# Queries of the second layer copied out into four buffers, and the out projection's weights asked for behind the first bias rows

## The chip, the cores and the metric

The kernel runs on one NeuronCore of a Trainium2 chip. The metric is the device time of one execution in microseconds (us). Three runs of the kernel before gave 2109.16, 2102.2 and 2106.66 us, median 2106.66 us.

## What is computed

The reference runs a model of two blocks over 1024 tokens of width 1024. The first block has an even layer (windowed attention and a state-space mixer) and an odd layer; a second block follows (state-space, convolution and a gated embedding). The change lies in the odd layer, called the second layer here:

```python
def odd_layer(hn, rel_bias, w_in, w_out, q_g, k_g):
    q, k, v, gate, qi, ki, wi = split_cols(hn @ w_in, ODD_SPLITS)
    q = rms_norm(q.reshape(bsz, L, C_HEADS, C_HEAD_DIM), q_g)
    k = rms_norm(k.reshape(bsz, L, C_KV_HEADS, C_HEAD_DIM), k_g)
    ...
    att = dsa_attention(q, k, v, qi, ki, wi, rel_bias)
    return (att * jax.nn.silu(gate)) @ w_out
```

There are 8 query heads and 2 key heads of 128. For each token a small indexer (qi, ki, wi) scores all earlier keys; the 256 best are kept, and the attention's logits (with a bias that depends on the distance) are masked to those. All of it is in float32.

## The kernel before

float32 products are made of three matmuls each on split operands (`mm3`, L146 to L150: high by high, high by low, low by high), so the lines L148, L149 and L150 come in threes on PE. Weights come in pieces of 128x512 (`wpiece`, L103): a load into one of three `wraw` buffers (L110, on SP), the high part by ACT (L122), the low part by POOL (L123). `wchunk` (L143) asks for eight of them.

The order of the instructions on each engine and of the DMAs on SP is found by the tile scheduler, which ranks what is ready by priority; `high_priority(offset=WPRIO)` lifts the weights' pieces (L106), the query loads (L1138) and the bias rows (L1164). Every engine, and SP as an issuer of DMAs, works through its list in order: what waits at its head holds all that is behind it.

The second layer (phase b, L835 to L1007) goes through these stages:

- Indexer scores into `sc2` to `sc7`, one row of scores for each block of 128 queries from the third on. Then the gate projection; its result goes through two buffers (tag "gt" in the pool `xp`, L926) to DRAM (`d_gate`). Then keys and values.
- The query projection (L958 to L967): two halves of 512 columns, eight token tiles each, 24 matmuls to a tile out of `hnTB`. After each tile comes `head_norm(..., leave=True)` (L400 to L410): ACT copies the PSUM bank out into `qo` (L401, two buffers, tag "qo"), squares its four heads (L404); POOL forms the reciprocal root and scales (L405, L168, L407) and stores the tile to `d_q` in DRAM (L409). A copy-out buffer is free again when its store has landed. In the second half the banks are three "tp" and one "mm" in turn (L963).
- Beside the query projection runs the choice of the 256 best (`TopK`): 31 steps of bisection. For the blocks 5, 6 and 7 a step is a small DVE operation (L1074), a Sign over the row of scores by ACT (L1078), and two small DVE operations (L1082, L1083). At the end DVE makes the mask (L1113 to L1123), a prefix scan (L1120) the longest piece of it.
- The pool `xp` is closed (L974) and `b_dsa_e` is opened over its space; `hnTB` is closed (L977), and `b_mix` (with `mixB`, L980), `b_ms` and `b_dsa` are opened over its space. So `mixB` waits for the last matmul that reads `hnTB`, and what lies in `b_dsa_e` waits for what lay in `xp`.
- The out projection's weights `wo` are asked for (L983), and the attention runs as a pipeline of 16 units, a block of queries by a key head (L985, blocks in the order 0, 1, 7, 6, 5, 4, 3, 2). A unit's `front` (L1149) loads its queries (`qf`, L1139, one buffer), turns them by four PE transposes (`tq`, L1143) into `qTB` (L1145 on ACT, L1146 on DVE), loads a row of biases for each of its four heads (`lgB`, L1165; the first two heads' buffers lie in `b_dsa_e`, the other two in `b_dsa`), makes the scores on PE (`s<-kTB,qTB`), adds the bias and takes the maximum on DVE (L1174), and normalises by ACT (L1178, L1180). Its `back` (L1183) transposes the weights (`tp`, L1192), multiplies by the values (`po`), loads the gate's 128x4x128 piece into `mixB` (L1199), and multiplies (L1200, DVE). The front of unit i+1 stands ahead of the back of unit i (L195 to L197).
- Both units of a block done, `out_tile` (L1010) splits `mixB` into `ms` (L1021, L1022), multiplies by `wo`, loads the block's 512 columns of x (`xr`, L1026, into the buffer with the tag "sq" that the squares of `head_norm` use), adds and stores.

Of the kernel before, what the change touches and what calls it, by code (L numbers as in the profile page):

```python
# [11 lines left out]
F32 = mybir.dt.float32  # L12
# [7 lines left out]
P = 128  # L20
# [32 lines left out]
def dap(ap, offset, pattern):  # L53
    return bass.AP(tensor=ap.tensor, offset=ap.offset + offset, ap=[list(p) for p in pattern])
# [135 lines left out]
def pipeline(att, units, done):  # L190

    late = None
    att.front(*units[0])
    for i, u in enumerate(units):
        if isinstance(att, DSA) and i + 1 < len(units):  # L195
            att.front(*units[i + 1])
        att.back(*u)  # L197
        if isinstance(att, SWA) and i + 1 < len(units):
            att.front(*units[i + 1])
        if late is not None:  # L200
            done(late)
            late = None
        if u[1] == 1:
            late = u[0]
    done(late)
# [183 lines left out]
def head_norm(k, pool, ps, nh, dh, dst, leave=False, o=None):  # L389

    nc = k.nc
    V, S, G = nc.vector, nc.scalar, nc.gpsimd
    n = nh * dh
    if o is None:
        o = pool.tile([P, 512], F32, tag="qo", name="qo", bufs=2)[:, :n]
    m = pool.tile([P, 16], F32, tag="hm", name="hm")
    r = pool.tile([P, 16], F32, tag="hr", name="hr")
    h3 = lambda a: a.rearrange("p (h d) -> p h d", h=nh)
    sq = pool.tile([P, 512], F32, tag="sq", name="sq", bufs=1)
    if leave:  # L400
        S.activation(o, ps, AF.Copy)  # L401
        for h in range(nh):
            hs = slice(h * dh, h * dh + dh)
            S.activation(sq[:, hs], o[:, hs], AF.Square, accum_out=m[:, h:h + 1])  # L404
        G.tensor_scalar(m[:, :nh], m[:, :nh], 1.0 / dh, 1e-6, op0=ALU.mult, op1=ALU.add)  # L405
        k.rstd(r[:, :nh], m[:, :nh], nh)
        G.tensor_tensor(h3(o), h3(o), r[:, :nh].unsqueeze(2).to_broadcast([P, nh, dh]), op=ALU.mult)  # L407
        if dst is not None:
            nc.gpsimd.dma_start(dst, o)  # L409
        return o  # L410
    S.activation(sq[:, :n], ps, AF.Square)
    V.tensor_reduce(m[:, :nh], h3(sq[:, :n]), axis=AX.X, op=ALU.add)
    V.tensor_scalar(m[:, :nh], m[:, :nh], 1.0 / dh, 1e-6, op0=ALU.mult, op1=ALU.add)
    k.rstd(r[:, :nh], m[:, :nh], nh)
    V.tensor_tensor(h3(o), h3(ps), r[:, :nh].unsqueeze(2).to_broadcast([P, nh, dh]), op=ALU.mult)  # L415
    if dst is not None:
        nc.sync.dma_start(dst, o)
    return o
# [416 lines left out]
def phase_b(k, x, hout, hB):  # L835
    hnT, sL = hB
    nc, tc, ins = k.nc, k.tc, k.ins
    V, S, G, T = nc.vector, nc.scalar, nc.gpsimd, nc.tensor
    W = ins["od_w_in"][0]
    d_q = tc.dram_tile([L, D], F32, name="d_q")  # L840
# [3 lines left out]
    gp = sR.enter_context(k.pool("b_g", side="right"))  # L844
# [11 lines left out]
    ps = k.tp()  # L856
# [8 lines left out]
    for th in range(2):  # L865
        cs = slice(th * 512, th * 512 + 512)
        ps = k.mm()
# [8 lines left out]
        ps = k.tp()  # L876
# [6 lines left out]
        for m in range(4):  # L883
            ps = k.mm()
# [5 lines left out]
            for e in range(2):  # L890
                a, b = slice(e * 64, e * 64 + 64), slice(64 - e * 64, 128 - e * 64)
# [8 lines left out]
    for b in range(2, 8):  # L900
        n = (b + 1) * P
# [18 lines left out]
    for ch in range(2):  # L920
        wg = k.wchunk(W, 1536 + ch * 512, 512)
        for m in range(4):
            for th in range(2):
                ps = k.mm()
                k.form2(ps, hnT, th * 512, wg, KT, m * P)
                gt = xp.tile([P, 512], F32, tag="gt", name="gtB", bufs=2)  # L926
# [15 lines left out]
    def keys(tt):  # L942
        ts_ = slice(tt * P, (tt + 1) * P)
        pt = k.tp()
        with tc.issue_after(k.last.ins):
            for j in range(2):
                T.transpose(pt[:, j * P:(j + 1) * P], kraw(tt)[:, j * P:(j + 1) * P], k.ident)
        src = pt[:, :256].rearrange("p (a t) -> p a t", a=2)
        S.activation(kT[:, 0, :, ts_], src, AF.Copy, scale=kg[:, 1:2])
        V.scalar_tensor_tensor(kT[:, 1, :, ts_], src, kg[:, 1:2], kT[:, 0, :, ts_].bitcast(F32),  # L950
                               op0=ALU.mult, op1=ALU.subtract)
    for tt in range(NT):
        ps = k.mm()
# [4 lines left out]
    for ch in range(2):  # L958
        wq = k.wchunk(W, ch * 512, 512)
        if ch:  # L960
            k.psum(mm=1,s=3,po=1,tp=3)
        for tt in range(NT):
            ps = k.ps(("tp", "tp", "tp", "mm")[tt % 4] if ch else "mm", "mm")  # L963
            k.form1(ps, hnT, tt * P, wq, KT, 512)
            if ch == 0:
                keys(tt)
            head_norm(k, gp, ps, 4, 128, d_q[tt * P:(tt + 1) * P, ch * 512:ch * 512 + 512], True)  # L967
    tks = [TopK(k, xp, sc, bs, act) for bs, act in TOPK]
    for bit in range(30, -1, -1):
        for t in tks:  # L970
# [7 lines left out]
    Wo = ins["od_w_out"][0]  # L978
    sL, (mp, mo) = stack(k.pool("b_mix"), k.pool("b_ms"))
    mix = mp.tile([P, 8, L], F32, name="mixB")  # L980
    with ExitStack() as c2:
        dp = c2.enter_context(k.pool("b_dsa"))
        wo = k.wchunk(Wo, 0, 512)  # L983
        ds = DSA(k, ep, dp, d_q, d_T, d_gate, kT, vB, sc, kg, mix)
        units = [(b, kv) for b in DORD for kv in range(2)]  # L985
        pipeline(ds, units, lambda b: out_tile(k, mo, gp, b, 0, [mix], wo, x, hout, "sq", 1))
    sR.close()
    k.wdve = WDVE[3]
# [10 lines left out]
    wo = [k.wpiece(Wo, kk, [(512, 512)], pool=op if kk < 4 else None, nx=4) for kk in range(KT)]  # L999
    for tt in range(NT):  # L1000
        h = out_tile(k, mo, op, tt, 1, [mix], wo, x, hout)
# [8 lines left out]
def out_tile(k, mo, p, tt, ch, mixes, w, x, hout, xtag="xr", nx=2, bank="mm"):  # L1010

    nc = k.nc
    V, S, G, T = nc.vector, nc.scalar, nc.gpsimd, nc.tensor
    ts_ = slice(tt * P, (tt + 1) * P)
    n = len(mixes)
    ps = k.ps(bank, "mm")
    for i in range(2):
        m = mo.tile([P, 2, 4, P], F32R, tag="ms", name="ms", bufs=MSB)
        with k.tc.high_priority(offset=2 * WPRIO if ch else 0):
            mx = mixes[i % n][:, (4 * i if n == 1 else 0):(4 * i if n == 1 else 0) + 4, ts_]  # L1020
            S.activation(m[:, 0], mx, AF.Copy)  # L1021
            (V if i and ((ch == 0 and tt == 7) or (ch == 1 and tt < 2)) else G).tensor_tensor(m[:, 1], mx, m[:, 0].bitcast(F32), op=ALU.subtract)  # L1022
        k.form1(ps, m, 0, w[4 * i:], 4, 512, start=i == 0, stop=i == 1)
    if ch == 0:
        xr = p.tile([P, 512], F32, tag=xtag, name="xr", bufs=nx)
        nc.sync.dma_start(xr, x[ts_, 0:512])  # L1026
    else:
        h = p.tile([P, D], F32, tag="hr", name="hr", bufs=3)
        nc.sync.dma_start(h[:, 0:512], hout[ts_, 0:512])
        nc.sync.dma_start(h[:, 512:], x[ts_, 512:])  # L1030
        xr = h[:, 512:]
    V.tensor_tensor(xr, ps, xr, op=ALU.add)
    nc.sync.dma_start(hout[ts_, ch * 512:ch * 512 + 512], xr)
    return None if ch == 0 else h
# [91 lines left out]
class DSA:  # L1126
# [22 lines left out]
    def front(self, b, kv):  # L1149

        k, p, kT = self.k, self.p, self.kT
        with k.tc.high_priority(offset=2 * WPRIO if b == DORD[0] else 0):
            qT = self.load(b, kv)
        nc = k.nc
        V, S, G = nc.vector, nc.scalar, nc.gpsimd
        n = (b + 1) * P
        st = p.tile([P, 5, 4], F32, tag="st", name="stB", bufs=3)
        hs, ts_ = slice(kv * 4, kv * 4 + 4), slice(b * P, (b + 1) * P)
        lgs = []
        for i in range(4):  # L1160
            h = kv * 4 + i
            lg = (self.pe if i < 2 else p).tile([P, L], F32, tag="lg", name="lgB", bufs=4)
            lgs.append(lg)
            with k.tc.high_priority(offset=WPRIO):  # L1164
                nc.sync.dma_start(lg[:, :n], dap(self.d_T, h * P * 1152 + 127 + P * (7 - b), [[1151, P], [1, n]]))  # L1165
            if b >= 2:
                G.tensor_tensor(lg[:, :n], lg[:, :n], self.masks[b], op=ALU.add)  # L1167
            mx = -3e38
            for j, c0 in enumerate(range(0, n, 512)):
                w = min(512, n - c0)  # L1170
                ps = k.ps("s")
                k.mm3(ps[:, :w], qT[:, 0, i], qT[:, 1, i], kT[:, 0, kv, c0:c0 + w], kT[:, 1, kv, c0:c0 + w],
                      True, True)
                V.tensor_tensor_reduce(lg[:, c0:c0 + w], ps[:, :w], lg[:, c0:c0 + w], 1.0, mx, ALU.add, ALU.max,  # L1174
                                       st[:, 3 + j, i:i + 1])
                mx = st[:, 3 + j, i:i + 1]
            V.tensor_scalar(st[:, 0, i:i + 1], mx, -1.0, None, op0=ALU.mult)
            S.activation(lg[:, :n], lg[:, :n], AF.Exp, bias=st[:, 0, i:i + 1], accum_out=st[:, 1, i:i + 1])  # L1178
            V.reciprocal(st[:, 2, i:i + 1], st[:, 1, i:i + 1])
            S.activation(lg[:, :n], lg[:, :n], AF.Copy, scale=st[:, 2, i:i + 1])  # L1180
        self.lgs[b, kv] = lgs
# [526 lines left out]
```

## Time and profile before

| what | value |
|---|---|
| median of 3 runs (lowest, highest) | 2106.66 us (2102.2, 2109.16) |
| the profiled execution's own time | 2105.1 us |
| its span in the trace | 2103.4 us, 27623 instructions |
| mean granted TensorE clock | 0.962 |
| busy PE / DVE / ACT / POOL | 92% / 69% / 43% / 44% |
| query projection, second half, to the attention's first units | some 820 to 900 us of the span |

The profiled execution took 2105.1 us of device time; its span in the trace, from the first instruction to the last, is 2103.4 us, and times in rows count from the span's start. A row of the timeline gives the start, the duration, the engine, the line, the operation with output and inputs, and in brackets how long the engine was idle before it and what ended that. PE's durations overlap (matmuls are pipelined), so idle times say more of PE than durations do.

### The profile page before, as it was taken

What the parts mean: (1) busy time and instruction counts of PE and PEld (TensorE: products, weight loads), DVE (VectorE), ACT (ScalarE), POOL (GpSimd) and SP (SyncE); (2) the same over time, 40 slices, a digit from 0 to 9 for tenths busy, and PEclk for the clock granted to TensorE, in tenths of its full rate; (3) what the DMA queues carried; (4) which work ended last, traced back from release to release, by engine and by line L of the source; (5) the groups of instructions that cost most, each with busy time, mean ns of one, the idle gap of its engine ahead of it and who ended that gap; (6) DMA issues with size and microseconds to landing.
All of it is one profiled execution on the core that took longest, in us unless ns stands there. A gap on an engine that the chain in (4) does not pass through costs nothing. (4 is left out here: it accounts for less than half of the span.)

```text
span 2103.4 us, 27623 instructions
## 1 busy us (share of the span) xinstructions
PE 1930.0 (92%) x9291; PEld 1565.0 (74%) x9291; DVE 1461.5 (69%) x2883; ACT 899.0 (43%) x1804; POOL 920.3 (44%) x774
## 2 busy tenths in 40 slices
PE   7988989989999998799988999999999559999998
PEld 6767767777888876677767788788888447778786
DVE  8465513584469988577646399999997588857737
ACT  5222326564456896677756211233322412144210
POOL 5476415545422246556457211222332576743204
PEclk9998999999999999899999999999999869999999
DMA  6543342313312212554355222223432435574442
GB/s 200 149 124 102 105 144 83 110 50 100 96 58 73 71 46 83 180 179 140 121 161 184 96 75 72 75 81 101 136 115 90 164 135 168 171 253 161 174 147 100
DMA packets 165671, 256.19 MB, mean 122 GB/s; under 512 B 29078, under 2 KB 77548, under 8 KB 165530
## 3 DMA queue, kind: packets, MB, share of 16 engines
q1 hardware_dynamic: 154026, 232.43, 34.5%
q10 hardware_dynamic: 10224, 17.82, 2.3%
q0 software_dynamic: 1280, 4.20, 0.5%
q8 instruction: 73, 1.20, 0.2%
q14 instruction: 68, 0.56, 0.1%
HBM read 185.35 MB, written 75.06 MB: 124 GB/s over the span
## 5 line engine op out<-in xcount | busy, mean ns | idle before, releaser
L123 POOL TENSOR_TENSOR w<-wraw,w 128x512 fp32r<-128x512 f32 (+1 forms) x230 | 314.8, 1384 | 657.2 <-ACT w L122 653.2
L1289 DVE SCALAR_TENSOR_TENSOR cy<-u,cw,cy 128x1024 f32<-128x1024 f32 x232 | 298.7, 1288 | 5.7
L122 ACT ACTIVATE w<-wraw 128x512 fp32r<-128x512 f32 (+1 forms) x230 | 141.2, 623 | 190.6 <-DMA wraw<-in_w_in_dram 54.7
L149 PE MATMUL mm<-hnTC,w 128*128 128x512 f32 (+1 forms) x336 | 131.6, 392 | 0.0
L150 PE MATMUL mm<-hnTC,w 128*128 128x512 f32 (+1 forms) x336 | 131.5, 391 | 0.0
L148 PE MATMUL mm<-hnTC,w 128*128 128x512 f32 (+1 forms) x336 | 131.5, 391 | 0.0
L150 PE MATMUL mm<-w,ms 128*128 128x512 f32 x256 | 106.0, 414 | 10.0 <-POOL ms L1022 8.5
L1167 POOL TENSOR_TENSOR lgB<-lgB,sc 128x1024 f32<-128x1024 f32 (+5 forms) x48 | 80.7, 1711 | 72.9 <-DMA lgB<-d_T 53.5
L148 PE MATMUL mm<-w,ms 128*128 128x512 f32 x256 | 104.9, 410 | 8.2 <-ACT ms L1021 8.1
L1078 ACT ACTIVATE tkj<-sc,tks 128x896 bf16<-128x896 f32 (+2 forms) x93 | 96.6, 1041 | 22.3 <-DVE tks L1074 19.5
L149 PE MATMUL mm<-w,ms 128*128 128x512 f32 x256 | 103.2, 403 | 0.0
L148 PE MATMUL mm<-w,hnTB 128*128 128x512 f32 x192 | 77.3, 404 | 11.9 <-ACT qo L401 8.9
L148 PE MATMUL mm<-w,hnTA 128*128 128x512 f32 (+1 forms) x192 | 73.3, 385 | 9.2 <-DVE qo L415 9.2
L148 PE MATMUL mm<-hnTB,w 128*128 128x512 f32 (+2 forms) x208 | 78.4, 377 | 0.3 <-ACT hnTB L172 0.3
L149 PE MATMUL mm<-hnTB,w 128*128 128x512 f32 (+2 forms) x208 | 78.1, 376 | 0.0
L150 PE MATMUL mm<-hnTB,w 128*128 128x512 f32 (+2 forms) x208 | 78.1, 375 | 0.0
L150 PE MATMUL mm<-w,hnTB 128*128 128x512 f32 x192 | 75.9, 396 | 0.0
L149 PE MATMUL mm<-w,hnTB 128*128 128x512 f32 x192 | 75.3, 395 | 0.0
L150 PE MATMUL mm<-w,hnTA 128*128 128x512 f32 (+1 forms) x192 | 73.4, 383 | 0.0
L149 PE MATMUL mm<-w,hnTA 128*128 128x512 f32 (+1 forms) x192 | 73.2, 382 | 0.0
L148 PEld LDWEIGHTS mm<-hnTC,w 128*128 128x128 f32 (+1 forms) x336 | 61.6, 183 | 14.5
L149 PEld LDWEIGHTS mm<-hnTC,w 128*128 128x128 f32 (+1 forms) x336 | 61.6, 183 | 14.4
(611 smaller groups left out, 5883.1 us busy)
## 6 DMA issues: line engine op xcount, KB each, us to landing
wraw<-in_w_in_dram SPq DMA_DIRECT2D x56, 256.0 KB
wraw<-in_od_w_in_dram SPq DMA_DIRECT2D x48, 256.0 KB
wraw<-in_ev_w_in_dram SPq DMA_DIRECT2D x32, 256.0 KB
wraw<-in_w_in_dram SPq DMA_DIRECT2D x64, 128.0 KB
wraw<-in_w_out_dram SPq DMA_DIRECT2D x32, 256.0 KB
ld<-d_cs SPq DMA_DIRECT2D x16, 512.0 KB
hr<-h SPq DMA_DIRECT2D x24, 256.0 KB
d_T<-d_row SPq DMA_DIRECT2D x8, 576.0 KB
```

Source lines behind the costliest of these rows:

```text
L122: nc.scalar.activation(t[:, 0, :o], raw[:, :o], AF.Copy)
L123: nc.gpsimd.tensor_tensor(t[:, 1, :o], raw[:, :o], t[:, 0, :o].bitcast(F32), op=ALU.subtract)
L148: mm(out, aH, bH, start=start, stop=False)
L149: mm(out, aH, bL, start=False, stop=False)
L150: self.last = mm(out, aL, bH, start=False, stop=stop)
L1078: S.activation(self.junk(n), sc[b], AF.Sign, bias=cand[:, i:i + 1], accum_out=cnt[:, i:i + 1])
L1167: G.tensor_tensor(lg[:, :n], lg[:, :n], self.masks[b], op=ALU.add)
L1289: V.scalar_tensor_tensor(py if i < 30 else y, u[:, i:i + L], cw[:, ct, i:i + 1], py, op0=ALU.mult, op1=ALU.add)
```

## The change

Two edits, and a third that serves the second. The odd tiles of the query projection are copied out into a tile `qg` of the pool `xp` with the tag "gt" (the gate projection's two buffers), the even ones go on using the two "qo" buffers. And `wo` is empty at first: after the front of the second unit its eight pieces are asked for inside `issue_after(ds.bias_load.ins)`, which holds them behind that unit's last bias load; for this `DSA.front` keeps the load's instruction.

```diff
             if ch == 0:
                 keys(tt)
-            head_norm(k, gp, ps, 4, 128, d_q[tt * P:(tt + 1) * P, ch * 512:ch * 512 + 512], True)
+            head_norm(k, gp, ps, 4, 128, d_q[tt * P:(tt + 1) * P, ch * 512:ch * 512 + 512], True,
+                      xp.tile([P, 512], F32, tag="gt", name="qg", bufs=2) if tt % 2 else None)
...
         dp = c2.enter_context(k.pool("b_dsa"))
-        wo = k.wchunk(Wo, 0, 512)
+        wo = []
         ds = DSA(k, ep, dp, d_q, d_T, d_gate, kT, vB, sc, kg, mix)
         units = [(b, kv) for b in DORD for kv in range(2)]
+        front = ds.front
+
+        def front_first(b, kv):
+            front(b, kv)
+            if (b, kv) == units[1]:
+                with tc.issue_after(ds.bias_load.ins):
+                    wo.extend(k.wchunk(Wo, 0, 512))
+        ds.front = front_first
         pipeline(ds, units, lambda b: out_tile(k, mo, gp, b, 0, [mix], wo, x, hout, "sq", 1))
...
             with k.tc.high_priority(offset=WPRIO):
-                nc.sync.dma_start(lg[:, :n], dap(self.d_T, h * P * 1152 + 127 + P * (7 - b), [[1151, P], [1, n]]))
+                self.bias_load = nc.sync.dma_start(lg[:, :n], dap(self.d_T, h * P * 1152 + 127 + P * (7 - b), [[1151, P], [1, n]]))
```

In the changed kernel the lines from L970 on stand one lower, those from L983 on nine lower (`qf` L1148, `tq` L1152, bias rows L1174, Sign L1087, `mixB` L1208, `xr` L1035).

The scheduler moves more than the two edits name. First SP's list of DMAs behind the last query weights (`wraw<-in_od_w_in_dram`), in the kernel before; `in_od_w_out_dram` is `Wo`:

```order
L110 DMA wraw<-in_od_w_out_dram 128x512 x8
L1139 DMA qf<-d_q 128x512
L1165 DMA lgB<-d_T 128x128 x4
L1139 DMA qf<-d_q 128x512
L110 DMA wraw<-in_od_w_out_dram 128x512 x2
L1165 DMA lgB<-d_T 128x128 x4
L1139 DMA qf<-d_q 128x512
L1199 DMA mixB<-d_gate 128x4x128
L110 DMA wraw<-in_od_w_out_dram 128x512
L1199 DMA mixB<-d_gate 128x4x128
L1165 DMA lgB<-d_T 128x256
```

And from the same place in the changed kernel:

```order
L1208 DMA mixB<-d_gate 128x4x128 x4
L1035 DMA xr<-h_77 128x512
L1208 DMA mixB<-d_gate 128x4x128 x12
L1148 DMA qf<-d_q 128x512
L1174 DMA lgB<-d_T 128x128 x8
L110 DMA wraw<-in_od_w_out_dram 128x512 x3
L1148 DMA qf<-d_q 128x512
L110 DMA wraw<-in_od_w_out_dram 128x512 x2
L1148 DMA qf<-d_q 128x512
L1174 DMA lgB<-d_T 128x256
```

All sixteen `mixB` loads and the first `xr`, which were spread over the first units, now stand ahead of the first `qf` and of every bias row; the weights stand behind the bias rows of the first two units. (In the kernel before the first eight are the pieces of `wo`; the two and the one further down belong to the projection's second half, L999.)

Then PE's list at the end of the query projection (`mm<-w,hnTB`) in the kernel before, around the transposes of the first unit's queries; from the last of these rows to the end of the projection nothing but its matmuls follows:

```order
L148 MATMUL mm<-w,hnTB 128x512
L149 MATMUL mm<-w,hnTB 128x512
L150 MATMUL mm<-w,hnTB 128x512
L1143 MATMUL tq<-ident,qf 128x128 x4
L148 MATMUL mm<-w,hnTB 128x512
```

And in the changed kernel at the end of the projection:

```order
L148 MATMUL mm<-w,hnTB 128x512
L149 MATMUL mm<-w,hnTB 128x512
L150 MATMUL mm<-w,hnTB 128x512
L1152 MATMUL tq<-ident,qf 128x128 x4
L148 MATMUL s<-kTB,qTB 128x128
L149 MATMUL s<-kTB,qTB 128x128
```

The first unit's transposes stood some three tiles ahead of the projection's end; now they stand behind its last matmul, directly ahead of the first scores.

Last ACT's list in the second half of the query projection, around the last Sign steps of block 7 (`tkj,tks<-sc`), in the kernel before:

```order
L1078 ACTIVATE tkj_7574,tks_7573<-sc_5067,tks_7573 128x1024 x2
L401 ACTIVATE qo<-mm 128x512
L404 ACTIVATE sq,hm<-qo 128x128 x4
L1078 ACTIVATE tkj_7574,tks_7573<-sc_5067,tks_7573 128x1024
L401 ACTIVATE qo<-mm 128x512
```

And in the changed kernel:

```order
L1087 ACTIVATE tkj_7574,tks_7573<-sc_5067,tks_7573 128x1024
L401 ACTIVATE qg<-mm 128x512
L404 ACTIVATE sq,hm<-qg 128x128 x4
L1087 ACTIVATE tkj_7574,tks_7573<-sc_5067,tks_7573 128x1024
L401 ACTIVATE qo<-mm 128x512
L1087 ACTIVATE tkj_7574,tks_7573<-sc_5067,tks_7573 128x1024
L404 ACTIVATE sq,hm<-qo 128x128 x4
L401 ACTIVATE qg<-mm 128x512
```

Where seven copies of the projection stood behind the last Sign step, five do now: two copies have moved ahead of it, and no two Sign steps stand together between copies.

## Rows read from the trace of the kernel before

**Rows 1.** The page, part 1 (PE's share) and part 2 (PE in 40 slices).

```profile
PE 1930.0 (92%) x9291; PEld 1565.0 (74%) x9291; DVE 1461.5 (69%) x2883; ACT 899.0 (43%) x1804; POOL 920.3 (44%) x774
...
PE   7988989989999998799988999999999559999998
```

**Rows 2.** Windows: stretch, length, busy PE, PEld, DVE, ACT, POOL, clock, DMA share, GB/s.

```profile
860.00:870.00 10.00, 3.10 (x22) 2.62 (x21) 0.79 (x6) 7.63 (x31) 8.07 (x11) 0.72 0.22 79
870.00:880.00 10.00, 7.30 (x36) 6.29 (x36) 5.55 (x31) 8.45 (x29) 4.92 (x7) 0.60 0.90 273
880.00:890.00 10.00, 6.70 (x28) 5.42 (x28) 4.51 (x18) 5.31 (x15) 2.57 (x2) 0.83 1.11 320
...
900.00:920.00 20.00, 19.14 (x97) 15.44 (x95) 14.65 (x46) 14.89 (x23) 17.42 (x9) 1.00 0.57 211
920.00:1040.00 120.00, 117.33 (x642) 95.36 (x640) 84.09 (x246) 91.28 (x162) 59.98 (x38) 1.00 0.38 128
```

**Rows 3.** Timeline of PE, the ends of its four long idle times and neighbours.

```profile
824.64 0.50 PE L148 MATMUL mm<-w,hnTB 128*128 128x512 f32 x1 [2.05 <-ACT qo L401]
...
837.27 0.79 PE L148 MATMUL mm<-w,hnTB 128*128 128x512 f32 x1 [6.89 <-ACT qo L401]
...
860.96 0.40 PE L150 MATMUL mm<-w,hnTB 128*128 128x512 f32 x1
861.19 0.22 PE L148 MATMUL s<-kTB,qTB 128*128 128x128 f32 x1
...
872.60 0.44 PE L148 MATMUL s<-kTB,qTB 128*128 128x128 f32 x1 [9.50 <-DVE stB L1174]
...
873.49 0.43 PE L1192 MATMUL tp<-ident,lgB 128*128 128x128 f32 x1
...
883.96 0.63 PE L1143 MATMUL tq<-ident,qf 128*128 128x128 f32 x4 [3.30 <-DMA qf<-d_q]
```

**Rows 4.** Timeline of ACT, copies, squares and Sign steps of the query projection's end.

```profile
835.49 1.15 ACT L1078 ACTIVATE tkj<-sc,tks 128x1024 bf16<-128x1024 f32 x1 [3.84 <-DVE tks L1074]
...
836.64 0.57 ACT L401 ACTIVATE qo<-mm 128x512 f32<-128x512 f32 x1
...
868.87 0.29 ACT L404 ACTIVATE sq<-qo 128x128 f32<-128x128 f32 x1
```

**Rows 5.** Timeline of SP's queue, loads of queries (L1139) and bias rows (L1165).

```profile
824.70 0.37 SPq L1139 DMA_DIRECT2D qf<-d_q  x1
825.16 31.00 SPq L1165 DMA_DIRECT2D lgB<-d_T  x4
856.33 0.32 SPq L1139 DMA_DIRECT2D qf<-d_q  x1
...
869.59 1.85 SPq L1165 DMA_DIRECT2D lgB<-d_T  x4
871.61 0.32 SPq L1139 DMA_DIRECT2D qf<-d_q  x1
```

**Rows 6.** Timeline of POOL, stores to d_q and a weight piece's low part (L123).

```profile
846.37 0.62 POOL L409 DMA_DIRECT2D d_q<-qo  x1 [0.30 <-POOL qo L407]
...
860.30 0.62 POOL L409 DMA_DIRECT2D d_q<-qo  x1 [0.30 <-POOL qo L407]
...
867.93 2.47 POOL L123 TENSOR_TENSOR w<-wraw,w 128x512 fp32r<-128x512 f32 x2
...
874.84 0.62 POOL L409 DMA_DIRECT2D d_q<-qo  x1 [0.30 <-POOL qo L407]
```

**Rows 7.** Tile mixB, its loads; tile qo, its stores from issue to landing.

```profile
L1199 SPq DMA_DIRECT2D mixB<-d_gate x16: 360/506/1557, 872.0 to 893.4; - x16
...
DMA to landing us min/median/max: 2.3/2.4/6.9
```

**Rows 8.** Windows, columns as in rows 2, of stretches in which loads crowd.

```profile
884.00:888.00 4.00, 4.00 (x16) 3.33 (x17) 2.52 (x11) 4.00 (x13) 1.54 (x2) 0.61 1.12 295
...
904.00:908.00 4.00, 4.00 (x24) 3.35 (x23) 3.23 (x10) 3.01 (x6) 4.00 (x3) 1.00 1.02 413
```

## The prediction

> **What bounds the kernel now.** I read the page first: PE is busy 92% of the span, and its line of slices is a row of 8s and 9s with a few dips [rows 1]. A slice is 52.6 us, so the digit 7 in the seventeenth covers 841 to 894 us, the place of this change. The windows come next: in 860 to 890 us PE works only 3.10, 7.30 and 6.70 us of each 10, while behind 920 it works 117.33 of 120 [rows 2]. So the attention is bound by PE once it runs, and a delay of its first units is passed on almost whole to the end of the span, as a gain is. What has to be costed is PE's idle time between 820 and 900 us.
>
> The timeline of PE has four long gaps there [rows 3]: 2.05 and 6.89 us inside the query projection, both ended by ACT's copy-out; 9.50 us after the first unit's scores, waiting for DVE, which lacked bias rows; 3.30 us for the third unit's queries. Together 21.74 us: all that this change can take away. The timeline of ACT says what the 6.89 us were [rows 4]: the copy of 836.64 stands right behind a Sign step that itself sat 3.84 us until DVE's top-k operation. At that place ACT did not lack a buffer; it stood, in order, behind the top-k.
>
> **Part one, four copy-out buffers.** No instruction is added: the same 16 copies and 16 stores have other destinations. By ACT's new order two copies move ahead of Sign steps, so the banks are emptied earlier. The gain lies between 0 (Sign steps hold ACT as before) and 8.94 us (2.05 + 6.89, both gaps gone). I keep 2 us of waiting, since three Sign steps still stand between copies and the copies of seven tiles become five behind the last one: a gain of 6.9 us. The last matmul of the projection then starts near 861 - 7 = 854 us.
>
> **Part two, the order on SP.** The bias rows no longer wait behind weights, so the 9.50 us gap as such goes; the 3.30 us one too, since the loads it competed with (`mixB`) are done by then. That is 12.8 us more. But the order shows what takes their place. Before, the first queries were issued at 824.70 and the second at 856.33, during the projection, and the first scores followed its last matmul after 0.23 us [rows 3, 5]. Now the first `qf` stands behind all sixteen `mixB` loads and one `xr`. The first `mixB` has to wait for the projection's last matmul (its space is `hnTB`'s), and `xr` for ACT's last square (same buffer tag). So nothing of the attention can be loaded while PE still projects, and PE stands idle from about 854 us until sixteen gate pieces have gone by. The price of that gap has three terms.
>
> First, the wait for ACT's last square, which holds SP at `xr`. It was 868.87 + 0.29 - 861.36 = 7.8 us behind the last matmul before [rows 3, 4], with three weight conversions and store waits in between; the least is one copy and four squares, 0.57 + 4 x 0.29 = 1.7 us [rows 4]. POOL's stores came (860.30 - 846.37) / 3 = 4.6 us apart [rows 6], and five tiles stand behind the last Sign step, so the tail does not vanish when PE is done sooner. I take 6 us, nearer the measured 7.8. Four `mixB` loads (1 MB) travel in this time and cost nothing; if the tail were 1.7 us they would cost about 2.
>
> Second, the transfer of what is left: `xr`, twelve `mixB` and `qf` are 14 loads of 256 KB, 3.67 MB, and the last queries' stores, some three of 256 KB, go at the same time. Where such loads crowd, the windows show 273 to 320 GB/s, 295 in the stretch with almost only gate pieces [rows 2, 8]; the most in this region is 413. Issue is no limit: 14 loads at a median of 0.506 us take 7.1 us [rows 7]. At 300 GB/s the loads take 12.2 us and the stores 2.6 us, 14.8 together. A landing follows, 2.4 us [rows 7]. The bounds: 3.67 MB at 413 GB/s, stores done already, 8.9 us; 4.46 MB at 273 GB/s, 16.3 us; the landing 2.3 to 6.9 us. So the gap is 6 + 14.8 + 2.4 = 23.2 us, between 13 and 31.
>
> The Trainium skill gives another price here ("DMA: Bandwidth & Descriptors", "Anatomy of one DMA — SWDGE (gpsimd) path"): a fixed 2.0 us and the bytes at 436 GB/s, fitted on another path than SP's. By that estimate the 4.46 MB would take 10.2 us, the gap 18.2 us and the whole change 5 us less; no row here reaches that rate, so the sum goes by 300.
>
> Third, the start of the pipeline, which was covered by the projection and no longer is. Query loads have one buffer, so the second `qf` is issued only behind the first transposes, and three weight loads and eight bias rows stand before it. Lightly loaded, a DMA lands in 2.3 us; the `qf` issued at 871.61 under load reached PE at 883.96, 12.3 us later [rows 3, 5, 7]. PE has the first unit's scores meanwhile (861.19 to 862.48, about 1.3 us, before), and DVE and ACT have to normalise alone. I take 8 us of idle time, between 2 and 12, nearer the loaded row since weights are moving then.
>
> **The weights' conversions** move too: eight low parts of 1.24 us (2.47 / 2), 10 us of POOL [rows 6], now in the first units. POOL works 2.57 of 10 us in 880 to 890 [rows 2], and the first out tile comes later by the gap as well, so I cost them at nothing; should that cover fail, the first out tile waits up to a few us. Taking three of them out of the projection's tail is in the 6 us above.
>
> **The sum.** Idle time before: 21.7 us. After: 2 + 23.2 + 8 = 33.2 us. That is 11.5 us more; I add 1 us because a PE that rested 23 us restarts at a lower granted clock, as it did here after its gaps (0.60 in 870 to 880, 0.83 in the next window [rows 2]); most of that is paid before as well. So +12.5 us: 2105.1 of the profiled execution becomes 2117.6, and, as that execution lies 1.6 us under the median of 2106.66, the median becomes **2119**. The bounds of all terms together: 0 + 13 + 2 - 21.7 = -7 us, and 9 + 31 + 12 - 21.7 = +30, all at their ends at once.
>
> **The rivals.** *Faster, near 2098.* Mechanism: the restart is short. If the tail is near 1.7 us and the crowd moves at 413 GB/s, the gap is 1.7 + 8.9 + 2.4 = 13 us and almost 1 more for the first four pieces, the start 2, no copy-out wait is left: -6 us. And the gate pieces, all in place early, would free the next units of their small waits, of which 900 to 920 us holds 0.86 and 920 to 1040 us 2.67 [rows 2]. For it: all four measured waits are really removed. Against it: no stretch with gate pieces passes 320 GB/s [rows 2, 8]. The point of decision is a first `tq` within 12 us after the last `mm<-w,hnTB`.
>
> *No change, near 2107.* A tail of 3 us, then 3.67 MB at 413 GB/s and 2.4 us of landing: 14.3 us; a start of 6 us, 1 us of copy-out waits, 21.3 against 21.7. The Trainium skill's figures (same page and section) with such a tail, 3 + 8.4 + 2.0 us, would give this case as well. Decided by a first `tq` 13 to 16 us behind the last matmul.
>
> *Much slower, near 2130.* Buffers do nothing because ACT stays behind the top-k (+7), or the tail is again 8 us and `qf` takes a landing of 6.9 us: 2 + 4.5 us more, and the start costs 12. Two of these make +20 to +24.
>
> *The change does not do what it says.* The copy-outs still wait for top-k, and the bias rows, though ahead of the weights, are late since they stand behind the gate pieces. Its first half is in the case above, its second half is my forecast.
>
> **How the numbers follow.** About 0.3%, 6.3 us, is what a measurement of this kernel can tell from no change. Forecast (+7 to +18): 0.62. Much slower: 0.17. No change: 0.13. Faster: 0.08. The range from 2106 to 2129 leaves out the upper part of the slow case and the faster one. Slower by over 0.3%: 0.78 (a part of the forecast's lower edge falls inside); same 0.14; faster 0.08.
>
> **What would show it.** Right: no copy-out wait of 6.89 us in the projection, its last matmul near 854; then one gap of PE of 20 us or more ended by `qf`, with the sixteen `mixB` loads ahead of it at about 300 GB/s; the first `tp` near 885 instead of 873.49; no wait for bias rows of 9.5 us; the attention behind it as long as before. Wrong: a gap under 16 us, a first `tp` at 875 or earlier, or later units that win back what the start lost.

## The result

The change makes the kernel slower: 2122.43 us median of four runs (2120.07 to 2123.64) against 2106.11 us (2102.2 to 2109.16), a ratio of 1.0077 with a 95% interval from 1.0064 to 1.009. That is 16.3 us more; 12.5 were forecast (a median of 2119), and 2122.4 lies in the range of 2106 to 2129. The profiled execution has a span of 2118.3 us, 14.9 more than before. PE is busy for the same time as before:

```profile
PE 1930.4 (91%) x9291; PEld 1565.3 (74%) x9291; DVE 1456.7 (69%) x2883; ACT 896.6 (42%) x1804; POOL 915.9 (43%) x774
```

It is the first line of the page after; against [rows 1] PE has 0.4 us more of work. So what was added is idle time. The timeline of PE after has the place; the bracket at a row's end is the idle time before it:

```profile
841.78 0.50 PE L148 MATMUL mm<-w,hnTB 128*128 128x512 f32 x1 [0.35 <-ACT qo L401]
...
852.56 0.39 PE L150 MATMUL mm<-w,hnTB 128*128 128x512 f32 x1
...
878.86 1.11 PE L1152 MATMUL tq<-ident,qf 128*128 128x128 f32 x4 [25.91 <-DMA qf<-d_q]
880.75 0.47 PE L148 MATMUL s<-kTB,qTB 128*128 128x128 f32 x1 [0.78 <-ACT qTB L1154]
...
885.01 1.08 PE L1152 MATMUL tq<-ident,qf 128*128 128x128 f32 x4 [1.44 <-DMA qf<-d_q]
887.83 0.77 PE L1201 MATMUL tp<-ident,lgB 128*128 128x128 f32 x2 [1.74 <-ACT lgB L1189]
```

The two stalls in the query projection are down to 0.35 us, and its last matmul starts at 852.56 instead of 860.96 [rows 3]: 8.4 us won. Then PE waits 25.91 us for the first queries; the scores, which followed the projection at once, start at 880.75 instead of 861.19. SP's queue after shows what the queries stood behind:

```profile
852.98 2.03 SPq L1208 DMA_DIRECT2D mixB<-d_gate  x4
862.64 0.33 SPq L1035 DMA_DIRECT2D xr<-h  x1
863.02 10.32 SPq L1208 DMA_DIRECT2D mixB<-d_gate  x12
873.45 1.04 SPq L1148 DMA_DIRECT2D qf<-d_q  x1
874.72 4.43 SPq L1174 DMA_DIRECT2D lgB<-d_T  x8
```

Four gate pieces go as soon as `hnTB` is free; then SP stands 7.6 us, for ACT's last square, as its waits say:

```profile
SPq L1035 <- ACT sq L404: 7.6, 1, 7.6
```

Twelve more pieces take 10.32 us to issue, and `qf`, issued at 873.45, reaches PE 5.4 us later. The tile's own row, which answers to [rows 7], has the same: all sixteen go out by 872.6, before any query.

```profile
L1208 SPq DMA_DIRECT2D mixB<-d_gate x16: 378/696/1379, 853.0 to 872.6; - x16
```

The windows after, columns as in [rows 2]:

```profile
860.00:870.00 10.00, 0.00 (x0) 0.00 (x0) 0.00 (x0) 1.28 (x8) 5.77 (x8) 0.50 0.72 211
870.00:880.00 10.00, 1.11 (x4) 0.71 (x4) 0.00 (x0) 0.00 (x0) 0.00 (x0) 0.50 1.09 284
880.00:890.00 10.00, 5.59 (x23) 4.63 (x24) 3.58 (x18) 7.64 (x19) 3.79 (x4) 0.50 0.65 202
890.00:900.00 10.00, 9.60 (x41) 8.31 (x42) 6.61 (x34) 8.49 (x26) 7.42 (x6) 0.52 0.81 245
900.00:910.00 10.00, 10.00 (x59) 8.60 (x58) 5.94 (x25) 8.44 (x25) 3.47 (x2) 1.00 0.61 212
```

From 860 to 870 PE does nothing at all. The clock is at its lower level, 0.50 (1.2 GHz), from 860 to 890, and at 0.52 on the mean until 900, longer than before, where it was 0.83 in 880 to 890 [rows 2].

To see what became of the loss I follow the multiplications by the gate (one to a unit, L1200, L1209 after). The first ended 12.57 us later than before (883.43 and 896.00), the last of the sixteen 14.70 us (1072.06 and 1086.76), and the span grew by 14.9: what is lost at the start of the attention is neither won back nor added to. From the first scores to that last multiplication the attention takes 206.01 us, before 210.87. So the account is: projection -8.40, gap before the scores +27.96 (28.19 behind the last matmul's start, 0.23 before), attention -4.86, together +14.70.

### The profile page after: what moved, and what is told of

Its sections match the earlier page's. It is cut to its first block, busy times and chain, and to the rows that moved or that the text cites. A ratio compares the mean times of both kernels' runs of the same rounds, so it can differ in the third digit from the quotient of the medians.

```text
span 2118.3 us, 27613 instructions
## 1 busy us (share of the span) xinstructions
PE 1930.4 (91%) x9291; PEld 1565.3 (74%) x9291; DVE 1456.7 (69%) x2883; ACT 896.6 (42%) x1804; POOL 915.9 (43%) x774
## 5 line engine op out<-in xcount | busy, mean ns | idle before, releaser
L123 POOL TENSOR_TENSOR w<-wraw,w 128x512 fp32r<-128x512 f32 (+1 forms) x230 | 311.2, 1368 | 684.8 <-ACT w L122 663.3
L1087 ACT ACTIVATE tkj<-sc,tks 128x896 bf16<-128x896 f32 (+2 forms) x93 | 96.7, 1044 | 27.1 <-DVE tks L1083 19.8
```

What stands on the lines that cost most here:

```text
L123: nc.gpsimd.tensor_tensor(t[:, 1, :o], raw[:, :o], t[:, 0, :o].bitcast(F32), op=ALU.subtract)
L1087: S.activation(self.junk(n), sc[b], AF.Sign, bias=cand[:, i:i + 1], accum_out=cnt[:, i:i + 1])
```

## The experiments

The prediction blamed SP's order: sixteen gate pieces and an `xr` ahead of the first queries. Rivals: the late weights cost (B), four buffers or the overlay of the gate buffers' space by the bias rows (C). Each kernel was timed in four rounds beside the kernel before, on the same chip in a group; the medians of the kernel before in the three groups were 2107.53, 2109.01 and 2108.69 us.

**The parts alone.** The first kernel has only the copy-out:

```diff
-            head_norm(k, gp, ps, 4, 128, d_q[...], True)
+            head_norm(k, gp, ps, 4, 128, d_q[...], True,
+                      xp.tile([P, 512], F32, tag="gt", name="qg", bufs=2) if tt % 2 else None)
```

> Part one alone: odd query tiles copied out into the gate projection's buffers, the out projection's weights asked for where they were before. Theory A (the order on SP: sixteen gate pieces and the first xr ahead of the first queries, which the late use of these buffers brings about): the order of the loads flips here too, so PE stands still over 20 us behind the query projection, and the time is 2114 to 2126 us. Rival B (the weights, asked for and converted late, are what costs): without them the time is 2098 or less, the projection's 8 us won and nothing lost.

Measured: 2128.39 us, ratio 1.01 [1.0079, 1.012]: 21 us slower than before. Its median lies 4 to 6 us above the whole change's in its two measurements, though the intervals of the ratios overlap. Its timeline of PE:

```profile
833.80 0.80 PE L148 MATMUL mm<-w,hnTB 128*128 128x512 f32 x1 [4.29 <-ACT qo L401]
...
889.61 1.12 PE L1144 MATMUL tq<-ident,qf 128*128 128x128 f32 x4 [31.15 <-DMA qf<-d_q]
```

SP's queue in the same kernel:

```profile
807.61 60.41 SPq L110 DMA_DIRECT2D wraw<-in_od_w_out_dram  x10
868.12 0.94 SPq L1200 DMA_DIRECT2D mixB<-d_gate  x2
...
870.67 13.65 SPq L1200 DMA_DIRECT2D mixB<-d_gate  x13
884.43 0.77 SPq L1140 DMA_DIRECT2D qf<-d_q  x1
```

The gate pieces stand ahead of the queries here too, so the copy-out alone turns the order; and with weights that wait for POOL still ahead of them, SP gets to the first piece only at 868.12. Rival B falls. Also, a stall of 4.29 us is left in the projection although it has four buffers (8.94 us in two stalls before); the copy that ends it stands behind a Sign step that had waited 6.33 us for the top-k.

The second kernel has only the weights' move (the `front_first` of the change, both copy-out buffers as before).

> Part two alone: two copy-out buffers as before, the weights behind the bias rows of the first two units. Theory A: queries and bias rows stand first in SP's list, the 9.5 us wait for bias rows and the 3.3 us wait for queries go, the projection keeps its two stalls: 2094 to 2099 us. Rival B (late weights cost): 2106 or more, with PE waiting for converted weights in the first out tile.

Measured: 2105.73 us, ratio 0.9998 [0.9984, 1.0013]: no change, where I expected 8 to 14 us of gain. The time alone is at the edge of rival B's (2106 or more), but PE waits only 0.5 us for a converted piece between 870 and 1090. One row of its windows:

```profile
820.00:840.00 20.00, 20.00 (x90) 16.38 (x89) 18.58 (x34) 8.99 (x28) 13.44 (x13) 1.00 0.12 44
```

Its timeline of PE:

```profile
857.11 1.09 PE L1151 MATMUL tq<-ident,qf 128*128 128x128 f32 x4 [1.05 <-DMA qf<-d_q]
868.46 0.48 PE L148 MATMUL s<-kTB,qTB 128*128 128x128 f32 x1 [10.26 <-ACT qTB L1153]
```

And of ACT:

```profile
857.98 0.60 ACT L401 ACTIVATE qo<-mm 128x512 f32<-128x512 f32 x1 [2.94 <-DMA d_q<-qo]
...
863.67 0.60 ACT L401 ACTIVATE qo<-mm 128x512 f32<-128x512 f32 x1 [3.73 <-DMA d_q<-qo]
...
865.66 1.28 ACT L1186 ACT_TABLE_LOAD   x1
```

Two things are new. The projection has no stall from 820 to 840, with two buffers: moving the eight weight pieces away from there takes both stalls, while four buffers alone took about half of them. How much of it is the conversions' own time on ACT and POOL, and how much the order of ACT's list, which moves with them, is not shown. And the wait for bias rows is gone, as both theories said, but 10.26 us of waiting for ACT stand in its place: ACT still copies the last tiles out, one after another as their buffers' stores land, and the first exponentials (behind the table load at 865.66) and the second unit's queries are in its list behind them. The projection is done 9.4 us sooner (its last matmul starts at 851.53), and the tail that was hidden beside it is laid open.

**The gate buffers, released early.** The whole change, but the last four tiles go through the old buffers:

```diff
-                      xp.tile([P, 512], F32, tag="gt", name="qg", bufs=2) if tt % 2 else None)
+                      xp.tile([P, 512], F32, tag="gt", name="qg", bufs=2) if tt % 2 and (ch == 0 or tt < 4) else None)
```

> Both parts, but the tiles 4 to 7 of the projection's second half go through the two old buffers, so the gate projection's buffers are last stored from some 30 us before the projection's end. Theory A: the queries and bias rows stay ahead of the gate pieces, the gains of both parts add up (8 us in the projection, 8 to 11 at the start of the attention): 2087 to 2094 us. Rival C (four buffers or late weights cost something by themselves): above 2100 us.

Measured: 2104.46 us, ratio 0.9976 [0.9962, 0.999], 3 to 5 us faster than before. Queries and bias rows stand first on SP again:

```profile
852.90 4.19 SPq L1174 DMA_DIRECT2D lgB<-d_T  x4
857.25 0.32 SPq L1148 DMA_DIRECT2D qf<-d_q  x1
```

And PE's long gap is gone:

```profile
855.21 0.33 PE L148 MATMUL s<-kTB,qTB 128*128 128x128 f32 x1 [2.50 <-ACT qTB L1154]
...
866.94 0.48 PE L148 MATMUL s<-kTB,qTB 128*128 128x128 f32 x1 [5.56 <-ACT qTB L1154]
...
872.27 0.47 PE L1201 MATMUL tp<-ident,lgB 128*128 128x128 f32 x1 [0.95 <-ACT lgB L1189]
```

Some 18 us lie between the medians of this kernel and the changed one (21 by their ratios, for they ran in different groups), for two tiles out of sixteen that use another buffer. The first theory holds as to the cause: the turned order comes from the late use of those buffers. That four buffers or late weights cost much by themselves falls, although the time is above the 2100 us that rival C named. But the gains don't add up to the 13 or more I expected: ACT's tail takes the rest, as in the kernel before this one.

**The order undone, the buffers kept.** Gate pieces, and `xr` of this stage, behind the latest bias rows:

```diff
-        k.nc.sync.dma_start(mx, self.d_gate[:, hs, ts_])
+        with k.tc.issue_after(self.bias_load.ins):
+            k.nc.sync.dma_start(mx, self.d_gate[:, hs, ts_])
...
-        nc.sync.dma_start(xr, x[ts_, 0:512])
+        with k.tc.issue_after(k.ds.bias_load.ins) if xtag == "sq" else ExitStack():
+            nc.sync.dma_start(xr, x[ts_, 0:512])
```

> All of the change, but gate pieces and the first xr are held behind bias rows by issue_after, so that the order on SP is again queries, bias rows, weights, gate pieces. It separates the order from the overlay: the first bias row still lies over both gate buffers and waits for their last store (issued at 866.1 in the changed kernel's trace). Theory A alone: the gap goes and both gains show: 2090 to 2096 us. Theory A with the overlay as a second cost: bias rows land near 871, the first tp comes near 874, as late as in the kernel before: 2105 to 2111 us. If neither order nor overlay is the cause: 2117 us or more.

Measured: 2108.22 us, ratio 0.9999 [0.9987, 1.001], the middle case. The order accounts for some 14 to 16 us. The overlay is the second cost, as the waits of SP show:

```profile
SPq L1176 <- DMA d_q<-qg: 78.5, 4, 51.8
```

SP's queue:

```profile
868.75 2.70 SPq L1176 DMA_DIRECT2D lgB<-d_T  x6
```

And PE's timeline:

```profile
871.13 0.47 PE L148 MATMUL s<-kTB,qTB 128*128 128x128 f32 x1 [5.57 <-DVE stB L1185]
```

The bias rows stand until 868.75 for the gate buffers' last store, 16 us behind `cut4`'s 852.90. In time this is worth less: 3.8 us between the two medians (2108.22 and 2104.46), 5 by the ratios.

**The terms of the gap.** With only one of the two edits above each, the tail (through `xr`) and the transfer are separated. First `xr` alone held back:

> The whole change, with only the first block's xr held behind bias rows: the sixteen gate pieces still stand ahead of the first queries, but nothing on SP waits for ACT's last square any more. Theory A (the gap is ACT's tail, 9.7 us, and then the transfer): the gate pieces go from 853 on, PE's gap shrinks from 25.9 to about 17 us, and the time falls by 7 to 10 us from the changed kernel's 2122: 2112 to 2116. Rival (transfer alone, the tail lies beside it): within 3 us of 2122.

Measured: 2122.14 us, ratio 1.0058 [1.0037, 1.0079]; the changed kernel, timed again in the same group, 2124.74. PE's timeline:

```profile
874.88 1.11 PE L1154 MATMUL tq<-ident,qf 128*128 128x128 f32 x4 [20.12 <-DMA qf<-d_q]
...
883.01 1.09 PE L1154 MATMUL tq<-ident,qf 128*128 128x128 f32 x4 [3.41 <-DMA qf<-d_q]
```

SP's queue in it:

```profile
854.80 13.82 SPq L1210 DMA_DIRECT2D mixB<-d_gate  x16
868.73 0.93 SPq L1150 DMA_DIRECT2D qf<-d_q  x1
873.65 3.65 SPq L1176 DMA_DIRECT2D lgB<-d_T  x8
```

The gap shrank by 5.8 us, to 20.12, not to 17, and the median by 2.6. Theory A's range was missed; the time is the rival's (within 3 us of 2122), though the gap did not stay as it was. The bias rows wait 3.7 us for the gate buffers' last store here:

```profile
SPq L1176 <- DMA d_q<-qg: 3.7, 1, 3.7
```

The second unit's queries stand behind these bias rows on SP, and PE waits 3.41 us for them, 1.44 in the changed kernel. The stores are late because they land late: the four issued from 857 to 868, beside the gate pieces, took 5.0, 6.0, 6.1 and 5.6 us to land; the same four in the next kernel, where no gate pieces stand in the way, 2.3, 2.6, 4.1 and 2.4. The tile `qg` from 840 to 890 has two of them, with two stores from before the crowd:

```profile
DMA to landing us min/median/max: 2.4/4.0/6.0
```

So the tail is not a plain term of the sum: take SP's wait for it away, and part of it comes back as a wait for the stores. Then the gate pieces alone held back:

> The whole change, with only the gate pieces held behind bias rows: the first xr, which waits for ACT's last square, still stands ahead of the first queries. Theory A: the gap of PE is the tail of 9.7 us and one landing, 12 to 14 us; bias rows wait for the gate buffers' last store as in both_late, so the time is near that one's, 2106 to 2112. Rival (the tail counts as much as the transfer): 2112 to 2116, as with xr_late.

Measured: 2106.21 us, ratio 0.9992 [0.9982, 1.0003]. PE's gap is the tail and a landing, 14.23 us:

```profile
869.21 1.12 PE L1152 MATMUL tq<-ident,qf 128*128 128x128 f32 x4 [14.23 <-DMA qf<-d_q]
```

The gate pieces ahead of the queries are worth 18.5 us (2124.74 to 2106.21), `xr` ahead of them 2.6 or less. The changed kernel beside both, the 2124.74 of that difference:

> The changed kernel itself beside these three on the same chip, so that differences of a few us are read against the same runs: 2120 to 2125 us.

It took 2124.74 us, ratio 1.008 [1.0063, 1.0098].

**An attempt to shorten ACT's tail.** `cut4` with POOL's two operations (L405, L407) of the last three tiles on DVE, the root still on POOL:

```diff
-        G.tensor_scalar(m[:, :nh], m[:, :nh], 1.0 / dh, 1e-6, op0=ALU.mult, op1=ALU.add)
+        X = V if leave == 2 else G
+        X.tensor_scalar(m[:, :nh], m[:, :nh], 1.0 / dh, 1e-6, op0=ALU.mult, op1=ALU.add)
...
-        G.tensor_tensor(h3(o), h3(o), r[:, :nh].unsqueeze(2).to_broadcast([P, nh, dh]), op=ALU.mult)
+        X.tensor_tensor(h3(o), h3(o), r[:, :nh].unsqueeze(2).to_broadcast([P, nh, dh]), op=ALU.mult)
...
+            head_norm(k, gp, ps, 4, 128, d_q[tt * P:(tt + 1) * P, ch * 512:ch * 512 + 512], 2 if ch and tt >= 5 else True,
...
```

> cut4 with the scaling of the projection's last three tiles on DVE instead of POOL (which took 3.6 us for a tile). If the start of the attention in cut4 is held by ACT's copies, which wait for POOL's chain and the stores, the last square comes 3 to 5 us sooner than cut4's 864 and the time is 2099 to 2102 us; if DVE, busy with the top-k until 854.6, holds them instead, the time is cut4's 2104 or more.

Measured: 2102.27 us, ratio 0.9975 [0.9961, 0.9989]. ACT's table load, which follows its last square, moved from 864.14 in `cut4` to 863.12, one us and not three to five. The projection's last matmul starts one us sooner as well (851.32 against 852.32), so ACT's tail behind it is as long as before, and the two ratios can't be told apart: this edit did not shorten the tail. Timed once more in the next group it gave 2103.25, ratio 0.9981 [0.9966, 0.9996]:

> The same kernel as cut4_dve5, beside the other two and the kernel before on one chip: 2100 to 2104 us, 5 to 7 us under the kernel before.

**Both, and the gate pieces spread out.** `cut4_dve5` with the two `issue_after` edits:

> cut4_dve5 with gate pieces and the first xr held behind bias rows as well. If what is left of PE's idle time at the start of the attention comes from loads that crowd (rates over 280 GB/s from 870 to 900 in cut4_dve5), spreading the gate pieces over the units gives another 1 to 4 us: 2098 to 2101. If it is ACT's order (squares, exponentials, conversions of weights), nothing: 2101 to 2104.

Measured: 2101.1 us, ratio 0.9965 [0.9951, 0.9979], 7.6 us under the kernel before in its group. It is the fastest median here; against `cut4_dve5_again` beside it (2103.25) 2 us, less than the intervals can tell apart.

**The clock.** 84 matmuls that nobody reads, between the projection and the first transposes (two other blocks, behind `issue_after(k.last.ins)` like this one, get the same `high_priority`; their lines are not shown):

```diff
+        idle = k.ps("po", "idle")
+        with tc.issue_after(k.last.ins), tc.high_priority(offset=10 * WPRIO):
+            for _ in range(84):
+                T.matmul(idle, kT[:, 0, 0, :P], kT[:, 0, 0, :512], start=True, stop=True)
...
```

> The whole change, with 84 matmuls whose result nobody reads (kT by kT, 128x512, into the po bank) between the query projection's last matmul and the first transposes of queries. They add work that nothing of the computation uses, in order to keep PE busy for some 19 of its 26 us of idle time; waits and loads stay as they are. In the changed kernel the clock is 0.50 from 860 to 900. If that low clock costs part of what the restart loses (theory: the first units' matmuls take twice as long, some 5 us more than idle times alone explain), the clock is 1.00 sooner and the time falls by 2 to 6 us below the changed kernel's, to 2117 to 2122. If the first units are held by waits for loads alone, the time stays within 1.5 us of it, 2122 to 2125.

Measured: 2122.85 us, ratio 1.0076 [1.0053, 1.0098], within 2 us of the changed kernel in its two measurements. It settles nothing, for the clock didn't stay up:

```profile
860.00:870.00 10.00, 10.00 (x46) 8.29 (x45) 0.00 (x0) 2.12 (x12) 6.56 (x10) 1.00 0.58 179
870.00:880.00 10.00, 3.20 (x15) 2.31 (x13) 0.00 (x0) 0.00 (x0) 0.00 (x0) 0.77 1.14 299
880.00:890.00 10.00, 4.81 (x20) 4.01 (x20) 2.11 (x12) 4.21 (x8) 3.72 (x3) 0.50 0.64 187
```

The queries came a little later, the added work ended 7.73 us ahead of them, and the clock was down again, at 0.50, when the first unit ran. The waits did not stay as they were either: ACT copies the first `qTB` behind two conversions of weights here, and PE waits 4.03 us for it, 0.78 in the changed kernel. What the lower clock costs stays open.

## Why the prediction held, and where it did not

*The gap behind the projection*, the main term, was right in cause and near in size: 23.2 us forecast, 25.9 measured. The tail was sized too short: 6 us taken, 9.7 measured (852.95, the end of the last matmul, to 862.64, the issue of `xr`); the transfer with its landing a little too long, 17.2 against 16.2 us from there to 878.86. The Trainium skill's figures ("DMA: Bandwidth & Descriptors", "Anatomy of one DMA — SWDGE (gpsimd) path") made 10.2 + 2.0 us of the same bytes, an estimate that this trace does not bear out; 284 GB/s moved in 870 to 880. "Issue is no limit" did not come out as written: SP took 10.8 us for `xr` and twelve pieces (862.64 to 873.45), 0.86 us a piece where the first four took 0.51, and `qf` reached PE 5.4 us after its issue. That SP was held up by transfers still under way fits the DMA share of 1.09 in 870 to 880 and is not shown by a run. `mixb_late` shows the cause: without the gate pieces in front, 18.5 us go. `xr_late` shows that adding a tail and a transfer was too simple, since stores land late beside gate pieces and the bias rows wait for them.

*The copy-out waits* went as forecast (8.6 of 8.94 us, 6.9 taken), but I gave the gain to the wrong part. The prediction put it to four buffers; `wo_late` has it with two buffers, `buf4` keeps 4.29 us with four. So the weights' move takes all of it by itself, the buffers about half.

*The gain of bias rows and queries* (12.8 us) was called a gain of the second part. Alone it is none: in `wo_late` 10.26 us of waiting for ACT's tail replace it. The prediction did not see that wait, since in the whole change it lies inside the gap of the queries. Within the whole change the account came out nearly right all the same: the attention, from its first scores on, was to win 12.8 - 8 - 1 = 3.8 us, and won 4.86. Its two parts were further off: PE's idle time in this stretch fell from 16.89 to 9.45 us, by 7.4 where 12.8 - 8 = 4.8 were forecast, so the start of the pipeline, taken as 8 us, was sized some 2.6 us too long. Some of the near hit is luck: the gap ahead of the scores came out 4.8 us above its forecast (27.96 against 23.2), the projection and the attention 1.5 and 1.1 us better than theirs.

*The lower clock* was given 1 us. PE's busy time from the first scores to the last multiplication rose from 193.98 to 196.56 us, 2.6, with the same matmuls. That this is the clock's doing fits the windows and is not shown by a run.

*The cover for the weights' conversions* held: behind 870 PE waits for no converted piece, in the first out tile or later up to 1090. The one such wait among PE's waits after, from 770 to 910, is that of a matmul at 813.50, inside the query projection:

```profile
PE mm L149 <- POOL w L123: 0.9, 1, 0.9
```

*The rivals.* "Faster" fell with the first `tq` 26 us behind the last matmul, "no change" with it. "Does not do what it says" was half right: the bias rows did come late, behind the gate pieces. "Much slower" had its long tail (9.7 us), but the copy-out waits went and `qf` landed in less than 6.9 us; its sum was off as well, for two of its prices on top of 12.5 make +23 to +26, not +20 to +24. And the loads with gate pieces did pass 320 GB/s before: 890 to 900, with four of them, moved 326.

## What to carry to other kernels

A borrowed buffer is paid for where its space is used next: the last use of a buffer in a pool that is about to close decides when everything over that space can start, and a scheduler that sees this reorders a whole queue, here for two late tiles out of sixteen. So borrow for the tiles that are early and give the space back before the next stage wants it, and read the order of every queue behind the change, not only of the lines that were touched. A wait that goes often uncovers another one just behind it (bias rows, then ACT's tail), so the gain of taking it away is the distance to the next wait, not its length.

## What was not expected of the hardware

Four stores of 256 KB that ran beside the gate pieces landed after 5.0 to 6.1 us in `xr_late`; without those pieces, in `mixb_late`, three of the four took 2.3 to 2.6 and one 4.1 us. And filling PE's wait with unread matmuls held the clock at 1.00 only while they ran (860 to 870); they ended at 873, and after 7.73 us without work it was at 0.50 in 880 to 890.
